# All rows for the attention's scores, and split activations on multiples of 512 bytes, in a two-layer hybrid decoder

## The chip, the cores and the metric

The kernel runs on one core of one Trainium2 chip. Times are device microseconds of one execution. A core has TensorE (PE: matmuls, and weight loads, PEld), VectorE (DVE), ScalarE (ACT), GpSimd (POOL) and SyncE (SP, which here only issues transfers). Each engine works through its own list of instructions in order and waits for others by semaphores.

## What is computed

Two layers, each of them three mixers over 512 tokens of width 1024 (x <- x + W_out(sum of gated projections)); the second mixer is the one whose scores change:

```python
def stick_breaking(q, k, v, q_norm, k_norm):          # 8 heads of 64, blocks of 128 queries
    q = rmsnorm(q, q_norm)
    k = rmsnorm(k, k_norm)
    for blk in range(S_ // SB_BLOCK):
        z = jnp.einsum('bqhd,bkhd->bhqk', q[:, start:end], k[:, :end]) * scale
        causal = s_idx[None, :] < t_idx[:, None]
        log_keep = jnp.where(causal, jax.nn.log_sigmoid(-z), 0.0)
        after = lax.cumsum(log_keep, axis=3, reverse=True) - log_keep
        w = jnp.where(causal, jnp.exp(jax.nn.log_sigmoid(z) + after), 0.0)
        outs.append(jnp.einsum('bhqk,bkhd->bqhd', w, v[:, :end]))

def hybrid_layer(x, ...):
    h = rmsnorm(x, norm_g)
    proj = h @ w_in                                    # 1024 x 8704, cut into 13 parts
    y_a = retention(...) * silu(rz);  y_b = stick_breaking(...) * silu(sz);  y_c = s5_ssm(...) * silu(cz)
    merged = sigmoid(ga) * (y_a @ proj_a) + sigmoid(gb) * (y_b @ proj_b) + sigmoid(gc) * (y_c @ proj_c)
    return x + merged @ w_out
```

## The kernel before

Large products are taken in a split form: a float32 value is the sum of a rounded float32r part (`hh`, `wh`, `yah`, ...) and the rest (`hl`, `wl`, `yal`, ...), and `three` (L336) adds the products high x high, high x low and low x high into one PSUM tile `mm`. The normalised, transposed input of a layer lies in two constant tiles, `hh` and `hl` (L235, L236; 128 partitions x 8 blocks x 512 tokens, so 16 KB of each partition). They are used in two ways:

- token-major (`token_major`, L351; `sq`, `sk`, `sv`, `cu`, `rq`, `rk`, `rv`): a block of 128 tokens of `hh` or `hl` is the stationary operand, a half of a weight tile `wh` or `wl` of 512 columns the moving one; 24 matmuls of 128x512 fill one tile. (`cu` takes every fourth token.)
- channel-major (`channel_major`, L371; gates `ga`, `gb`, `gc`, and `sz`, `cz`, `rz`): 128 columns of a weight are stationary, and the 512 tokens of `hh` or `hl` move; again 24 matmuls.

In the profile a matmul is named out<-moving,stationary, so `mm<-wh,hh` is token-major and `mm<-hh,wh` channel-major. The projections `pa`, `pb`, `pc` and the output product have tiles of the pool in place of `hh` and `hl` (`yah`, `ybh`, `ych`, `mgh`).

The program is written slot by slot: the table `ORDER_TEXT` gives the order of the main pieces, of 24 or 12 matmuls each, and small work (the attention's heads, the state-space quarters, the retention chunks) is put between the pieces by generators that say after how many slots they go on (`K`). Background work that builds the state-space tables is added by a running count of each engine's load.

An attention pair `sb_pair` (L1015) holds two heads of 64 rows each, one in partitions 0 to 63 and one in 64 to 127. Its first slot splits queries and keys: `qd` is the rounded query, copied by POOL to the other half of the partitions; `ks` holds the rounded key in the head's half and the key's rest in the other, so that one 128-row product `qd x ks` gives high x high plus high x low; `ql`, one tile for both heads, is the query's rest, and its product with the rounded key has 64 rows. `scores` (L1032) puts these two and a bf16 mask product (`identb x negm`) into PSUM; the first block (b = 0) takes one product of the unsplit float32 queries and keys over 64 rows, which PE runs as two instructions. Block 3 has a slot of its own (tile `z3`); blocks 0, 2 and 1 are one run in a later slot (`z02` and `z1`). Behind them ACT takes two sigmoids, DVE scans and multiplies (`weights_of`, L1043), and PE transposes the weights (`turn`, L1061, tile `wt`). The next pair's split comes in the slot of a pair's last run of three blocks.

The tiles of the large pool (`bt`, L216, 48 buffers of 2 KB) are handed out again as they come free.

Of the kernel before, what the change touches and what calls it, by code (L numbers as in the profile page):

```python
# [10 lines left out]
F32 = mybir.dt.float32  # L11
F32R = mybir.dt.float32r
BF16 = mybir.dt.bfloat16
AF = mybir.ActivationFunctionType
ALU = mybir.AluOpType
PSUM = bass.MemoryType.PSUM

P = 128
L = 2
S = 512  # L20
# [166 lines left out]
def trunk(ctx: ExitStack, tc, x_in, w_in, par_in, bc_in, ng_in, cst_in, rope_in, out):  # L187
    nc = tc.nc
    load = {"V": 0.0, "G": 0.0, "T": 0.0}

    def counted(f, engine, each):


        def g(*a, **k):
            o = k["out"] if "out" in k else a[0]
            load[engine] += 0.07 * (engine != "T") + each * math.prod(o.shape[1:])
            return f(*a, **k)  # L197

        return g

    TT = counted(nc.vector.tensor_tensor, "V", 1.04e-3)
# [4 lines left out]
    MM = counted(nc.tensor.matmul, "T", 0.42e-3)  # L206

    const = ctx.enter_context(tc.tile_pool(name="const", bufs=1))
# [7 lines left out]
    def bt(name, dt=F32, shape=(P, 512)):  # L216
        return bp.tile(list(shape), dt, tag="b", name=name)
# [7 lines left out]
    def psm(name):  # L225
        return ps_sm.tile([P, 512], F32, tag="sm", name=name)
# [3 lines left out]
    ident = const.tile([P, P], F32, name="ident")  # L230
    identb = const.tile([P, P], BF16, name="identb")
    negm = const.tile([P, P], BF16, name="negm")
    mhalf = const.tile([P, 32], F32, name="mhalf")
    zero1 = const.tile([P, 1], F32, name="zero1")
    hh = const.tile([P, 8, S], F32R, name="hh")  # L235
    hl = const.tile([P, 8, S], F32R, name="hl")  # L236
    x1 = dp.tile([S, D], F32, name="x1")

    def C(n):
# [7 lines left out]
        out=negm, in_=negm, pattern=[[1, P]], base=0, channel_multiplier=-1, compare_op=ALU.is_ge, fill=0.0  # L247
# [31 lines left out]
    def split(src, name, shape=(P, 512)):  # L279
        h = bt(name + "h", F32R, shape)  # L280
        l = bt(name + "l", F32R, shape)
        ACT(h, src, AF.Copy)  # L282
        TT(out=l, in0=src, in1=h.bitcast(F32), op=ALU.subtract)
        return h, l
# [523 lines left out]
    def layer(l, last, base):  # L808
# [206 lines left out]
        def sb_pair(pr):  # L1015
            w02, w3 = [None] * 2, [None] * 2
            qf, kf = sq[pr], sk[pr]
            half = [slice(0, 64), slice(64, 128)]

            qd = [bt("qd0", F32R), bt("qd1", F32R)]  # L1020
            ks = [bt("ks0", F32R), bt("ks1", F32R)]
            ql = bt("ql", F32R)
            for h in range(2):
                r, o = half[h], half[1 - h]
                ACT(qd[h][r, :], qf[r, :], AF.Copy)  # L1025
                ACT(ks[h][r, :], kf[r, :], AF.Copy)
                TT(out=ql[r, :], in0=qf[r, :], in1=qd[h][r, :].bitcast(F32), op=ALU.subtract)
                TT(out=ks[h][o, :], in0=kf[r, :], in1=ks[h][r, :].bitcast(F32), op=ALU.subtract)
                nc.gpsimd.tensor_copy(out=qd[h][o, :], in_=qd[h][r, :])  # L1029
            yield K["b1"]  # L1030

            def scores(ps, off, h, b):  # L1032
                n = 128 * (b + 1)
                c = slice(b * P, b * P + P)
                r = half[h]
                if b == 0:
                    MM(ps[:, off : off + n], qf[r, c], kf[r, 0:n], start=True, stop=False)
                else:
                    MM(ps[:, off : off + n], qd[h][:, c], ks[h][:, 0:n], start=True, stop=False)
                    MM(ps[:, off : off + n], ql[r, c], ks[h][r, 0:n], start=False, stop=False)  # L1040
                MM(ps[:, off + n - P : off + n], identb, negm, start=False, stop=True)

            def weights_of(ps, segs, sg):  # L1043

                end = sum(segs[-1])
                kp = bt("kp")
                ACT(kp[:, 0:end], ps[:, 0:end], AF.Sigmoid, scale=-0.125)  # L1047
                ACT(sg, ps[:, 0:end], AF.Sigmoid, scale=0.125)
                for off, n in segs:
                    v = kp[:, off + 1 : off + n][:, ::-1]  # L1050
                    nc.vector.tensor_tensor_scan(v, v, zero1.to_broadcast([P, n - 1]), 1.0, ALU.mult, ALU.add)  # L1051
                TT(out=sg[:, 0 : end - 1], in0=sg[:, 0 : end - 1], in1=kp[:, 1:end], op=ALU.mult)

            w1 = bt("w1")
            wt0, wt13, wt2 = [None] * 2, [None] * 2, bt("wt2")

            def wblk(h, b, kb):
                c = kb * P + (128 if b == 2 else 256 * h if b == 1 else 0)
                return (w02[h], w1, w02[h], w3[h])[b][:, c : c + P]

            def turn(h):  # L1061
                pts = []
                for blocks in (
                    [(b, 0) for b in range(4)], [(1, 1), (2, 1), (3, 1), (3, 3)], [(2, 2), (3, 2)],
                ):
                    pt = psm("wt")
                    for i, (b, kb) in enumerate(blocks):
                        nc.tensor.transpose(pt[:, i * P : i * P + P], wblk(h, b, kb), ident)
                    pts.append(pt)
                return pts  # L1070

            def turned(h, pts):
                wt0[h], wt13[h] = bt("wt0"), bt("wt13")
                ACT(wt0[h], pts[0], AF.Copy)
                nc.vector.tensor_copy(out=wt13[h], in_=pts[1])
                ACT(wt2[:, 256 * h : 256 * h + 256], pts[2][:, 0:256], AF.Copy)

            for h in range(2):
                ps = psm("z3")
                scores(ps, 0, h, 3)  # L1080
                if h == 1:
                    pts = turn(0)
                yield 0
                w3[h] = bt("w3")
                weights_of(ps, [(0, 512)], w3[h])
                if h == 1:
                    turned(0, pts)
                yield K["b2"]
                ps, ps1 = psm("z02"), psm("z1")
                scores(ps, 0, h, 0)  # L1090
                scores(ps, 128, h, 2)
                scores(ps1, 0, h, 1)
                yield 0
                w02[h] = bt("w02")
                weights_of(ps, [(0, 128), (128, 384)], w02[h])
                weights_of(ps1, [(0, 256)], w1[:, 256 * h : 256 * h + 256])
                yield K["b3"]
            pts = turn(1)
            yield 0
            turned(1, pts)  # L1100
            yield K["b4"]
            po = psm("sbo")
            for kb in range(4):

                for h in range(2):
                    c = slice(128 * pr + 64 * h, 128 * pr + 64 * h + 64)
                    w = (wt0[h], wt13[h][:, 0:384], wt2[:, 256 * h : 256 * h + 256], wt13[h][:, 384:512])[kb]
                    MM(po[half[h], 128 * kb : 512], sv[kb][:, c], w, start=kb == 0, stop=kb == 3)
            yield 0
            sbo[pr] = bt("sbo")  # L1110
            nc.vector.tensor_copy(out=sbo[pr], in_=po)
            yield K["b5"]
            while zb[pr] is None:
                yield 1
            TT(out=sbo[pr], in0=sbo[pr], in1=zb[pr], op=ALU.mult)
            yb[pr] = split(sbo[pr], "yb")
# [207 lines left out]
        for i in range(4):  # L1324
            spawn(sb_pair(i), at["sv"] + 3 + K["sb0"] + K["sb_gap"] * i)
# [66 lines left out]
```

## Time and profile before

| what | value |
|---|---|
| median of 3 runs (range) | 1330.12 us (1329.44 to 1330.89) |
| the profiled execution: its time, its span | 1332.1 us, 1330.4 us |
| PE busy | 1299.4 us, 98% |
| DVE busy | 854.5 us, 64% |
| ACT busy | 537.7 us, 40% |
| POOL busy | 371.3 us, 28% |
| PE clock granted, mean | 0.993 |

Busy time counts from an instruction's start to its end. PE's matmuls overlap each other, so their rows add up to more than the time they take; the distance from one start to the next is what a matmul costs in a stream. Idle time in front of a row is named with the engine that ended it. Buffer numbers are left out of names, so `z` stands for `z3`, `z02` and `z1`, `ks` for `ks0` and `ks1`, `sqk` for the unsplit queries and keys.

### The profile page before, as it was taken

The numbers are of one execution on the slowest core, as the hardware profiler recorded it, in microseconds if no ns is written. First come the engines' busy times: TensorE is split into PE (matmuls) and PEld (weight loads), VectorE is DVE, ScalarE is ACT, GpSimd is POOL, SyncE is SP. The second block draws the span as 40 slices with busy tenths as digits, with TensorE's granted clock in tenths as the row PEclk, the third lists the DMA queues.
The fourth block names the chain that finished last, engine by engine and source line by source line (L and its number), as shares of the span: only waits on it lengthen the run. The fifth ranks groups of instructions, "written<-read, shape, count | busy, mean of one in ns | idle before, by whom it ended". The sixth has DMA issues, their size and how long they took to land. (4 is left out here: it accounts for less than half of the span.)

```text
span 1330.4 us, 16615 instructions
## 1 busy us (share of the span) xinstructions
PE 1299.4 (98%) x6360; PEld 1051.4 (79%) x6360; DVE 854.5 (64%) x1189; ACT 537.7 (40%) x919; POOL 371.3 (28%) x436
## 2 busy tenths in 40 slices
PE   7989989999999999999999999899999999999998
PEld 5867768788887888888888777688888878888887
DVE  5996677886686438555365566779647854485542
ACT  5345543535434434333234444344544444333311
POOL 3330035738443012000052000575465321120000
PEclk9999989999999999999999999899999999999999
DMA  6232221223321222224533221112242233223342
GB/s 220 85 125 77 64 64 30 94 68 96 100 91 64 95 80 73 86 91 139 166 113 125 79 65 64 48 64 80 80 127 64 64 94 97 79 64 95 95 131 75
DMA packets 37375, 120.05 MB, mean 90 GB/s; under 512 B 4144, under 2 KB 4528, under 8 KB 37296
## 3 DMA queue, kind: packets, MB, share of 16 engines
q1 hardware_dynamic: 29664, 105.40, 25.2%
q10 hardware_dynamic: 7632, 13.59, 3.0%
q8 instruction: 50, 0.82, 0.3%
q14 instruction: 29, 0.24, 0.1%
HBM read 114.78 MB, written 4.19 MB: 89 GB/s over the span
## 5 line engine op out<-in xcount | busy, mean ns | idle before, releaser
L197 DVE TENSOR_TENSOR wl<-raw,wh 128x1024 fp32r<-128x1024 f32 x196 | 250.4, 1287 | 122.1 <-ACT wh L316 120.0
L197 PE MATMUL mm<-hh,wh 128*128 128x512 f32 x640 | 256.7, 401 | 0.0
L197 PE MATMUL mm<-hh,wl 128*128 128x512 f32 x640 | 252.4, 394 | 2.3 <-DVE wl L197 2.3
L197 PE MATMUL mm<-hl,wh 128*128 128x512 f32 x640 | 250.5, 391 | 0.0
L316 ACT ACTIVATE wh<-raw 128x1024 fp32r<-128x1024 f32 x196 | 206.0, 1057 | 86.1 <-DVE wl L197 31.1
L197 PE MATMUL mm<-wh,hh 128*128 128x512 f32 x512 | 210.2, 411 | 0.9 <-ACT hh L419 0.9
L197 PE MATMUL mm<-wl,hh 128*128 128x512 f32 x512 | 205.3, 401 | 4.1 <-DVE wl L197 4.1
L197 PE MATMUL mm<-wh,hl 128*128 128x512 f32 x512 | 204.7, 400 | 0.0
L197 PEld LDWEIGHTS mm<-hh,wl 128*128 128x128 f32 x640 | 120.6, 188 | 30.3 <-DVE wl L197 3.6
L197 PEld LDWEIGHTS mm<-hh,wh 128*128 128x128 f32 x640 | 120.8, 189 | 24.9 <-issue 1.8
L197 PEld LDWEIGHTS mm<-hl,wh 128*128 128x128 f32 x640 | 120.7, 189 | 24.5
L197 PEld LDWEIGHTS mm<-wl,hh 128*128 128x128 f32 x512 | 104.8, 205 | 25.7 <-DVE wl L197 6.8
L197 PEld LDWEIGHTS mm<-wh,hh 128*128 128x128 f32 x512 | 104.6, 204 | 21.3 <-ACT hh L419 1.3
L197 PEld LDWEIGHTS mm<-wh,hl 128*128 128x128 f32 x512 | 104.5, 204 | 20.9 <-DVE hl L197 0.3
L1051 DVE TENSOR_TENSOR_SCAN kp<-kp,zero 128x511 f32<-128x511 f32 (+1 forms) x64 | 60.3, 963 | 35.6 <-ACT kp L1047 35.1
L992 ACT ACTIVATE gate<-mm 128x512 f32<-128x512 f32 x48 | 28.6, 596 | 119.7 <-PE mm L197 119.7
L197 POOL TENSOR_SCALAR ms<-ss 128x8 f32<-128x8 f32 (+3 forms) x56 | 19.2, 342 | 184.0 <-DVE ss L822 101.9
L1029 POOL CAST qd<-qd 64x512 fp32r<-64x512 f32 x16 | 15.8, 988 | 186.9 <-ACT qd L1025 172.0
L197 POOL TENSOR_TENSOR rs<-ms,mhalf 128x8 f32<-128x8 f32 (+3 forms) x56 | 64.7, 1155 | 4.7
L820 ACT ACTIVATE sq<-mm 128x512 f32<-128x512 f32 x32 | 19.0, 593 | 89.1 <-PE mm L197 89.1
L197 PE MATMUL mm<-wl,mgh 128*128 128x512 f32 x128 | 50.1, 391 | 0.2
L197 PE MATMUL mm<-wh,mgh 128*128 128x512 f32 x128 | 49.9, 390 | 0.0
(254 smaller groups left out, 2260.4 us busy)
## 6 DMA issues: line engine op xcount, KB each, us to landing
raw<-in_w SPq DMA_DIRECT2D x196, 512.0 KB, 3.5
x<-in_x SPq DMA_DIRECT2D x8, 256.0 KB, 7.3
rope<-in_rope ACTq DMA_DIRECT2D x8, 256.0 KB, 4.3
xh<-in_x ACTq DMA_DIRECT2D x8, 256.0 KB, 4.6
x<-xh ACTq DMA_DIRECT2D x8, 256.0 KB, 2.1
xh<-x ACTq DMA_DIRECT2D x8, 256.0 KB, 4.5
out<-xh ACTq DMA_DIRECT2D x8, 256.0 KB, 2.1
gB<-in_ng SPq DMA_DIRECT2D x2, 256.0 KB, 5.8
```

The source lines that it names most:

```text
L197: return f(*a, **k)
L316: ACT(wh, raw, AF.Copy)
L820: ACT(s2, ps, AF.Square)
L992: ACT(sg, ps, AF.Sigmoid)
L1029: nc.gpsimd.tensor_copy(out=qd[h][o, :], in_=qd[h][r, :])
L1051: nc.vector.tensor_tensor_scan(v, v, zero1.to_broadcast([P, n - 1]), 1.0, ALU.mult, ALU.add)
```

## The change

Two things are done. First, `ql` becomes two tiles, one per head; POOL sets the half of each that the head doesn't use to zero, and all scores, those of block 0 too, are `qd x ks` and `ql x ks` over 128 rows. Second, two unused tiles are put among the constants, and `hh` and `hl` come ahead of the two small ones.

```diff
     negm = const.tile([P, P], BF16, name="negm")
+    const.tile([P, 152], F32, name="fill")
+    hh = const.tile([P, 8, S], F32R, name="hh")
+    hl = const.tile([P, 8, S], F32R, name="hl")
     mhalf = const.tile([P, 32], F32, name="mhalf")
     zero1 = const.tile([P, 1], F32, name="zero1")
-    hh = const.tile([P, 8, S], F32R, name="hh")
-    hl = const.tile([P, 8, S], F32R, name="hl")
+    const.tile([P, 104], F32, name="fill2")
...
-            ql = bt("ql", F32R)
+
+            ql = [bt("ql0", F32R), bt("ql1", F32R)]
             for h in range(2):
                 r, o = half[h], half[1 - h]
                 ACT(qd[h][r, :], qf[r, :], AF.Copy)
                 ACT(ks[h][r, :], kf[r, :], AF.Copy)
-                TT(out=ql[r, :], in0=qf[r, :], in1=qd[h][r, :].bitcast(F32), op=ALU.subtract)
+                nc.gpsimd.memset(ql[h][o, :].bitcast(F32), 0.0)
+                TT(out=ql[h][r, :], in0=qf[r, :], in1=qd[h][r, :].bitcast(F32), op=ALU.subtract)
...
-                r = half[h]
-                if b == 0:
-                    MM(ps[:, off : off + n], qf[r, c], kf[r, 0:n], start=True, stop=False)
-                else:
-                    MM(ps[:, off : off + n], qd[h][:, c], ks[h][:, 0:n], start=True, stop=False)
-                    MM(ps[:, off : off + n], ql[r, c], ks[h][r, 0:n], start=False, stop=False)
+                MM(ps[:, off : off + n], qd[h][:, c], ks[h][:, 0:n], start=True, stop=False)
+                MM(ps[:, off : off + n], ql[h][:, c], ks[h][:, 0:n], start=False, stop=False)
                 MM(ps[:, off + n - P : off + n], identb, negm, start=False, stop=True)
```

In the built program `hh` began at byte 18,496 of a partition and `hl` at 34,880, both 64 bytes past a multiple of 512; now they begin at 18,944 and 35,328, which are multiples of 512. The weight and activation pools lay 1,024 bytes past multiples of 2,048 and now lie on multiples of 2,048; multiples of 512 they were before, too.

On PE, the run of blocks 0, 2 and 1 of the first head of layer 1 (`z_1054` and `z_1059` are the tile of blocks 0 and 2). Before:

```order
L197 MATMUL z_1054<-sqk 128x128
```

and now:

```order
L197 MATMUL z_1059<-ks_949,qd_947 128x128
L197 MATMUL z_1059<-ks_949,ql_951 128x128
```

Every run of three blocks, 16 in all, has these two in place of the one; the rest of PE's list stands as it was, with `ql` read over 128 rows.

On POOL, the quarter of the state-space tables in which block products with `ccr` and `cci` are built (`ct`, then `ca`, then the copies `b` and the cleared `mt`); what an instruction waits for stands behind it. Before:

```order
L197 TENSOR_TENSOR ct_1930<-ccr,y_re 128x512 [waits PE_49]
L197 TENSOR_TENSOR ct_1931<-cci,y_im 128x512 [waits Pool_49]
L197 TENSOR_TENSOR ca<-ct_1930,ct_1931 128x4x128 [waits Pool_49]
L763 COPY b_1997<-bbr 64x256
L763 COPY b_1997<-bbi 64x256 [waits Pool_49]
```

and now:

```order
L197 TENSOR_TENSOR ct_1951<-ccr,y_re 128x512 [waits PE_49,Activation_49]
L197 TENSOR_TENSOR ct_1952<-cci,y_im 128x512 [waits DVE_49]
L197 TENSOR_TENSOR ca<-ct_1951,ct_1952 128x4x128 [waits Pool_49]
L765 COPY b_2018<-bbr 64x256 [waits DVE_49]
L765 COPY b_2018<-bbi 64x256 [waits Pool_49]
```

The order is the same; the second `ct` and the first `b` have other buffers than before, which DVE has to release. In POOL's list 16 memsets are new, each directly ahead of the copy of `qd` of the same head.

## Rows read from the trace of the kernel before

**Rows 1.** The page, busy time of PE: us, share of the span, instructions.
```profile
PE 1299.4 (98%) x6360; PEld 1051.4 (79%) x6360; DVE 854.5 (64%) x1189; ACT 537.7 (40%) x919; POOL 371.3 (28%) x436
```
**Rows 2.** PE's waits: who waited for whom, us in total, times, longest.
```profile
PE wt L1068 <- DVE w L197: 8.1, 4, 2.4
PE mm L197 <- DVE wl L197: 6.3, 7, 1.5
PE z L197 <- DVE ks L197: 2.7, 1, 2.7
```
**Rows 3.** PE's timeline, blocks 0, 2, 1 of a head: start us, us, operation.
```profile
180.50 0.40 PE L197 MATMUL mm<-hh,wl 128*128 128x512 f32 x1
...
181.28 0.42 PE L197 MATMUL z<-ks,qd 128*128 128x384 f32 x1
181.63 0.44 PE L197 MATMUL z<-ks,ql 64*128 64x384 f32 x1
...
182.65 0.23 PE L197 MATMUL z<-negm,identb 128*128 128x128 bf16 x1
...
183.01 0.40 PE L197 MATMUL mm<-hl,wh 128*128 128x512 f32 x1
```
**Rows 4.** PE's timeline, block 3 of the other head; in brackets idle time, releaser.
```profile
188.28 0.40 PE L197 MATMUL z<-ks,qd 128*128 128x512 f32 x1
188.61 0.50 PE L197 MATMUL z<-ks,ql 64*128 64x512 f32 x1
189.04 0.23 PE L197 MATMUL z<-negm,identb 128*128 128x128 bf16 x1
...
193.64 1.76 PE L1068 MATMUL wt<-ident,w 128*128 128x128 f32 x7 [2.41 <-DVE w L197]
```
**Rows 5.** The chain that ended last: start us, us from start to next, instructions.
```profile
1078.62 5.60 PE mm L197 x24
...
1112.27 0.89 PE rs L197 x8
...
1124.16 0.72 PE ro L197 x6
...
1192.03 5.50 PE mm L197 x24
...
1233.57 49.08 PE mm L197 x216
```
**Rows 6.** Timelines of DVE and PE behind the first pair's last scores.
```profile
123.46 0.42 DVE L197 TENSOR_TENSOR w<-w,kp 128x255 f32<-128x255 f32 x1
...
124.29 1.26 PE L1068 MATMUL wt<-ident,w 128*128 128x128 f32 x10
```
**Rows 7.** The page, costliest groups of PE: count | busy us, mean ns | idle.
```profile
L197 PE MATMUL mm<-wh,hh 128*128 128x512 f32 x512 | 210.2, 411 | 0.9 <-ACT hh L419 0.9
...
L197 PE MATMUL mm<-wh,mgh 128*128 128x512 f32 x128 | 49.9, 390 | 0.0
...
L197 PE MATMUL mm<-hh,wh 128*128 128x512 f32 x640 | 256.7, 401 | 0.0
L197 PE MATMUL mm<-hl,wh 128*128 128x512 f32 x640 | 250.5, 391 | 0.0
```
**Rows 8.** POOL's groups with shapes apart: the nearest memset.
```profile
L767 POOL MEMSET mt<- 128x512 f32 x16 | 7.9, 526 | 0.5
```
**Rows 9.** Timelines of POOL, DVE and PE at a quarter of the tables.
```profile
212.39 1.51 POOL L197 TENSOR_TENSOR ct<-cci,y_im 128x512 f32<-128x512 f32 x1
...
216.44 0.75 POOL L763 COPY b<-bbi 64x256 f32<-64x256 f32 x1
...
216.97 0.77 DVE L197 TENSOR_TENSOR Ti<-ct,ct 128x512 f32<-128x512 f32 x1
...
224.13 0.64 PE L197 MATMUL pk<-ca,b 128*32 128x128 f32 x16
```
**Rows 10.** Stretch: us, busy of PE, PEld, DVE, ACT, POOL, PE clock, DMA.
```profile
188.00:196.00 8.00, 3.93 (x16) 2.96 (x16) 7.70 (x6) 3.26 (x6) 6.83 (x6) 0.80 0.22 66
```

## The prediction

> **What bounds the kernel now.** I read the page's busy table first: TensorE (PE) is busy 1299 us of the span of 1330 [rows 1]. A busy PE is not a PE at its peak, so next came its waits: besides the start these are the transposes of the attention's weights (`wt`, 8.1 us in all), the layer's products `mm` (6.3 us) and the first scores `z` of layer 1 (2.7 us), all waiting for VectorE (DVE) [rows 2]. So nearly every nanosecond taken from a PE instruction shortens the span, except just before those waits. After that I read PE's start-to-start times in the timeline, since each matmul starts before the one ahead has drained: the length of a row is not its cost, the distance to the next start is.
>
> **The scores, as they stand.** For a head the blocks 0, 2 and 1 are one run of PE work. From the start of the last `mm` ahead (180.50) to the start of the second `mm` behind (183.01) are 2.51 us [rows 3]; two `mm` of 0.227 us (price below) are not the scores', so the run costs 2.05 us. Inside it every change between a 128-row and a 64-row product shows as lost time: the 384-column product over 128 rows begins at 181.28 and the one over 64 rows behind it only at 181.63, 0.35 us later. Block 3 is a second run: its 512-column product starts at 188.28, the 64-row one at 188.61, the mask at 189.04, so two products take 0.76 us [rows 4]. Both runs come 16 times (2 layers, 4 pairs, 2 heads).
>
> **What they cost with all rows.** Now all products have 128 rows and nothing is switched inside a run. Prices by column count come from the chain of work that ended last, in which PE instructions follow each other without a gap: 512 columns 0.227 us, 256 columns 0.72/6 = 0.12 us, 128 columns 0.89/8 = 0.11 us [rows 5]; 384 columns lie between, about 0.17 us. A mask costs what 182.65 to 183.01 leaves after one `mm`, 0.13 us [rows 3], less where the product ahead is short; I take 0.11 us. The run of three blocks is then 2 x 0.11 + 2 x 0.17 + 2 x 0.12 + 3 x 0.11 = 1.13 us, 0.92 us less, x16 = **14.7 us**. Block 3 is 2 x 0.227 in place of 0.76 us: 0.30 us less, x16 = **4.8 us**. Raw sum 19.5 us.
>
> The unknown price is the 128-column product of float32r, of which the trace has none. Below: at the rate of the 512-column row it streams in 0.06 us, which would gain another 32 x 0.05 = 1.6 us; above: a four-byte float32 product of 128 columns is two instructions of 0.11 us [rows 5], and if float32r needs both, 32 x 0.11 = 3.5 us are lost. I take 0.11 us, since that row is such an instruction, with a load of the same size in front.
>
> **What of it is lost again.** The weights' transposes wait for DVE's chain behind the scores. Where the next pair's split comes in between, this chain starts with ScalarE's work on the `mm` piece that ends before the scores, so shorter scores do not shorten it. In the third such place PE already waits (193.64, after 2.41 us) [rows 4]: the whole 1.2 us goes, in both layers, 2.4 us. In the first such place DVE ends `w` at 123.88 and PE starts `wt` at 124.29 [rows 6]: 0.4 us of cover, so 0.8 us is lost there, and the same in the second; four in all, 3.2 us. The stop at layer 1's first `z` takes 0.3 us, and later `mm` stops for `wl` [rows 2] I put at 0.6 us. Scores net: 19.5 - 6.5 = **13 us**.
>
> **The places of `hh` and `hl`.** In token-major products these are the stationary operand, in channel-major ones the moving one. A token-major piece of 24 takes 5.60 us, 0.2333 each; a channel-major piece 5.50 us, 0.2292 each; the 216 that follow are one such piece and 192 products of the `pa` projection, whose operands all lie on multiples of 512 bytes: (49.08 - 5.50)/192 = 0.2270 each [rows 5]. The mean durations lean the same way: 411 ns with stationary `hh`, 390 with stationary `mgh`, 401 with moving `hh` [rows 7]. There are 3 x 512 token-major and 3 x 640 channel-major products on `hh`, `hl`. At full effect: 1536 x 6.3 ns = 9.7 us and 1920 x 2.2 ns = 4.2 us. PE's gain on `sk`, `sq` and `sv` of layer 1 (288 products, 1.8 us) ends at the DVE wait before the first `z`, and some 100 products before the `wl` stops of each layer give 1.2 us more away. Of the 10.9 us left I take three quarters, **8 us**, because the `pa` stretch is long and unbroken, while pieces on `hh` are often cut by transposes, behind which the pace need not be as good. Ends: nothing, and 11 us.
>
> For the size of this a page of the Trainium skill can be set beside the row. Even the `pa` row keeps 0.227 us for 512 columns [rows 5]. TensorE: Matmul & The Clock Gate, section "Back-to-back issue gap", gives N/2.4 + 2.5 ns, 0.216 us for 512 columns at the full clock; if alignment brought that, an estimate from this page, the gain would be 1536 x 17 + 1920 x 13 ns = 51 us. The aligned products of this trace do not run so, and I follow the row.
>
> **What is added.** GpSimd (POOL) gets 16 memsets of 64 x 512. The nearest row is a memset of 128 x 512 at 0.53 us [rows 8]; POOL stands idle before most of the copies beside which they come, and nobody waits for POOL's copies. Cost 0, at most 16 x 0.5 = 8 us were POOL the bound. DVE's and ScalarE's lists do not change. The second `ql` takes one more buffer of the pool per pair, so later tiles get other buffers: in the quarter of the state-space tables that stands at 212.39 [rows 9], POOL's `ct` now reuses a buffer that DVE reads until 217.74. POOL stops there for up to 5.4 us, with `ca`, `b` and `mt` queued behind it, and PE's `pk` (224.13) waits for these. From 212.39 to the end of `b` (217.19) are 4.8 us; begun at 217.74 they end at 222.5, 1.6 us ahead of `pk`, and PE comes earlier by about the 1.2 us of a head's scores. I take 0; both layers have the place.
>
> **Sum.** 13 + 8 = 21 us. The profiled execution took 1332.1 us (span 1330.4, 1.7 around it), 2 us above the median of the runs, 1330.1; I take the difference from both, and forecast **1309 us** for the median.
>
> **Rivals.**
> - *Alignment does nothing.* `hh` and `hl` differ from the `pa` operands in more than the offset: they lie in another part of the memory, and the matmuls around them differ. For it: a moving `hl` shows no loss, 391 ns against 401 for `hh` at the same offset [rows 7]. Then only the scores count: 1330 - 13 = 1317 us. SBUF — State Buffer, section "Specifications (TRN2)" in the Trainium skill, speaks for this rival: full rate needs two hits per 16-byte line, and 64 bytes past a boundary is the start of such a line. No run here shows the lines by themselves.
> - *The scores' gain stays in DVE's chains.* If the other weights' transposes, too, have less cover than I think, half the scores' gain goes: 1330 - 6 - 8 = 1316; with alignment at nothing 1324 us. Against: PE stops for `w` in few places [rows 2].
> - *Slower: POOL's new stop reaches PE.* If `pk` waits, PE stands still, and behind a stop of this size the granted clock falls: in the 8 us around the stop at 189 it is 0.80, where the levels are 1.2 and 2.4 GHz [rows 10]. A stop of 5.4 us in each layer with some 2 us of low clock costs 15 us. That ends slower only where alignment gives nothing and the scores give under 12 us: 1330 - 12 + 15 = 1333 us. It decides from 6 us of stop per layer on. Against: the copies to be waited for end before `pk` even with the stop.
>
> **How the numbers follow.** Forecast 0.60 (1309), alignment nothing 0.22 (1317), chains 0.12 (1316 to 1324), slower 0.03 (1333), no effect of size 0.03. Range: from 1303 (alignment 11, scores 13, the short products at 0.06 us, and a little less lost) to 1321 (alignment nothing, short products at the dear price 1317 + 3.5). A measurement here tells about 0.2% (2.7 us) from no change. Faster 0.94, same 0.03, slower 0.03.
>
> **What would show it.** The distance from the last `mm` ahead of a three-block run to the second behind should fall from 2.51 to about 1.6 us, and no 0.35 us step between products should remain; 128-column products starting 0.21 us apart would be the dear price. A token-major piece should take 5.45 us in place of 5.60, a channel-major one 5.46 in place of 5.50. The stop at 193.64 should be longer by about 1 us, and new short waits of `wt` for `w` should appear. A wait of `pk` for POOL, or a slower `pa`, would prove me wrong; unchanged 5.60 would make the first rival's case, and a fall well below 5.45 would mean that more than the offset cost time.

## The result, and the profile after

The changed kernel takes **1310.67 us** (median of 4 runs, 1309.67 to 1311.17) against 1330.17 us for the kernel before on the same chip: a ratio of 0.985, 95% interval 0.9835 to 0.987, or 19.5 us less. The forecast was 1309 us. The profiled execution has a span of 1309.5 us.

The page of the changed kernel, busy time, answers to [rows 1].

```profile
PE 1271.7 (97%) x6360; PEld 1048.5 (80%) x6360; DVE 855.6 (65%) x1189; ACT 537.6 (41%) x919; POOL 382.5 (29%) x452
```

PE's waits (who waited for whom, us in total, times, longest) answer to [rows 2].

```profile
PE wt L1068 <- DVE w L197: 13.5, 8, 3.1
PE mm L197 <- DVE wl L197: 9.2, 7, 3.3
PE T L398 <- DVE xn L197: 9.0, 2, 7.4
PE mm L197 <- ACT hh L421: 0.9, 1, 0.9
PE z L197 <- DVE ks L197: 0.8, 1, 0.8
```

PE is busy 28 us less and waits more: its waits were 26.9 us in all and are now 33.4 us. `wt` now waits for `w` in 8 places, not 4, and for 5.4 us more. So PE's own work fell by more than the time did, and part of it came back as waiting.

PE's timeline of the changed kernel at the first run of blocks 0, 2 and 1 of layer 1 (start us, us, operation) answers to [rows 3], which show a later run of the kernel before:

```profile
99.75 0.39 PE L197 MATMUL mm<-hh,wl 128*128 128x512 f32 x1
99.98 0.22 PE L197 MATMUL z<-ks,qd 128*128 128x128 f32 x1
100.03 0.28 PE L197 MATMUL z<-ks,ql 128*128 128x128 f32 x1
100.15 0.23 PE L197 MATMUL z<-negm,identb 128*128 128x128 bf16 x1
100.19 0.42 PE L197 MATMUL z<-ks,qd 128*128 128x384 f32 x1
100.45 0.34 PE L197 MATMUL z<-ks,ql 128*128 128x384 f32 x1
...
100.99 0.23 PE L197 MATMUL z<-negm,identb 128*128 128x128 bf16 x1
101.03 0.48 PE L197 MATMUL mm<-hh,wh 128*128 128x512 f32 x1
101.35 0.40 PE L197 MATMUL mm<-hl,wh 128*128 128x512 f32 x1
```

From 99.75 to 101.35 are 1.60 us, where 2.49 to 2.51 stood before, depending on the run. The 384-column product over 128 rows is followed by the next one 0.26 us later, in place of 0.35. The two products of 128 columns start 0.06 us apart.

PE's timeline at the place of [rows 4], a block 3 with the transposes of the attention's weights behind it (idle time and its releaser in brackets); this is the third such place of layer 1:

```profile
181.93 0.39 PE L197 MATMUL z<-ks,qd 128*128 128x512 f32 x1
...
182.39 0.23 PE L197 MATMUL z<-negm,identb 128*128 128x128 bf16 x1
185.68 0.30 PE L1068 MATMUL wt<-ident,w 128*128 128x128 f32 x1 [3.07 <-DVE w L197]
188.40 2.18 PE L1068 MATMUL wt<-ident,w 128*128 128x128 f32 x9 [2.41 <-DVE w L197]
```

Two products take 0.46 us in place of 0.76. The first `wt` now starts 3.30 us behind the mask. Before it was 1.89 us (the mask at 189.04 in [rows 4], `wt` at 190.93):

```profile
190.93 0.30 PE L1068 MATMUL wt<-ident,w 128*128 128x128 f32 x1 [1.66 <-DVE w L197]
```

So this stop is 1.4 us longer; the second stop, the one that [rows 4] show, kept its 2.41 us.

The chain that ended last (start us, us to the next, instructions) answers to [rows 5]:

```profile
1058.78 5.49 PE mm L197 x24
...
1171.24 5.49 PE mm L197 x24
...
1212.72 49.02 PE mm L197 x216
```

One of the page's groups (count, busy us, mean ns, idle) answers to [rows 7]:

```profile
L197 PE MATMUL mm<-wh,hh 128*128 128x512 f32 x512 | 207.5, 405 | 0.9 <-ACT hh L421 0.9
```

The token-major piece at 1058.78 went from 5.60 to 5.49 us, the channel-major one at 1171.24 only from 5.50 to 5.49 (other channel-major pieces of the chain fell further, see below); the 192 products of `pa` behind a piece of 24 still take (49.02 - 5.49)/192 = 0.2267 us each. With stationary `hh` the mean duration fell from 411 to 405 ns.

### The profile page after: what moved, and what is told of

The parts are those of the page before. It is cut to its first block, busy times and chain, and to the rows that moved or that the text cites. A ratio compares the mean times of both kernels' runs of the same rounds, so it can differ in the third digit from the quotient of the medians.

```text
span 1309.5 us, 16640 instructions
## 1 busy us (share of the span) xinstructions
PE 1271.7 (97%) x6360; PEld 1048.5 (80%) x6360; DVE 855.6 (65%) x1189; ACT 537.6 (41%) x919; POOL 382.5 (29%) x452
## 5 line engine op out<-in xcount | busy, mean ns | idle before, releaser
L197 PE MATMUL mm<-wh,hh 128*128 128x512 f32 x512 | 207.5, 405 | 0.9 <-ACT hh L421 0.9
L197 PE MATMUL mm<-wl,hh 128*128 128x512 f32 x512 | 202.6, 396 | 4.3 <-DVE wl L197 4.3
L197 PE MATMUL mm<-wh,hl 128*128 128x512 f32 x512 | 202.0, 395 | 0.0
L1051 DVE TENSOR_TENSOR_SCAN kp<-kp,zero 128x511 f32<-128x511 f32 (+1 forms) x64 | 67.6, 1076 | 26.2 <-ACT kp L1047 26.1
```

## The experiments

Each run is compared with runs of the kernel before on the same chip (medians of 1330.0, 1330.0 and 1331.1 us in the three groups of runs, 1330.2 beside the changed kernel). Where a run is set against the changed kernel instead, these differences of up to 1 us stand between the two.

### The two halves alone

`e_scores` has the second half of the diff only, `e_place` the first only:

```diff
 e_scores
-            ql = bt("ql", F32R)
+            ql = [bt("ql0", F32R), bt("ql1", F32R)]
...
 e_place
+    const.tile([P, 152], F32, name="fill")
+    hh = const.tile([P, 8, S], F32R, name="hh")
+    hl = const.tile([P, 8, S], F32R, name="hl")
...
+    const.tile([P, 104], F32, name="fill2")
```

> The scores' change alone: all products over 128 rows, hh and hl where they were (64 bytes past a multiple of 512). Theory (two gains that add): the scores are worth 11 to 13 us net, so 1317 to 1319 us; three-block runs last 1.60 us, a token-major piece of 24 stays at 5.60 us and a channel-major one at 5.50. Rival (the scores did nearly all, and the place of hh and hl only adds waits later): 1312 us or less. Rival (most of the scores' gain is lost before DVE's chains, and the places carry the result): 1322 us or more.

> The places of hh and hl alone (18,944 and 35,328), scores as before. Theory: the token-major piece falls to 5.49 us, the channel-major one by 0.01, together 8 us: 1322 us. Rival (alignment does nothing by itself): 1329 to 1331 us. If e_scores and this one together give clearly more than 19.5 us, the two parts compete for the same waits; if less, they help each other.

Measured: the scores alone 1316.87 us (1316.46 to 1318.41; ratio 0.9905, interval 0.989 to 0.9919), 13.2 us less than before; the places alone 1322.81 us (1322.06 to 1324.12; ratio 0.9948, interval 0.9933 to 0.9963), 7.2 us less. Together 20.4 us, where the whole change gave 19.5: the halves add up to within 1 us, and both of the forecast's terms, 13 and 8, hold.

### Which operand's place counts, and by how much

The forecast read the loss as "64 bytes past a multiple of 512" and left open that the region of memory or the neighbours were the cause. Six runs move the tiles of the changed kernel by a few bytes and change nothing else: `fill` moves `hh` and `hl`, and `fill2` takes up the difference or, where it doesn't, moves all tiles of the pools (weights, `yah`, `mgh` and so on). The diff is that of `e_off32`; the others have other numbers in these two lines (first column of numbers in the table below).

```diff
-    const.tile([P, 152], F32, name="fill")
+    const.tile([P, 160], F32, name="fill")
...
-    const.tile([P, 104], F32, name="fill2")
+    const.tile([P, 96], F32, name="fill2")
```

> The changed kernel with hh and hl moved by 64 bytes (19,008 and 35,392), everything else at the same addresses. Theory (the offset from a multiple of 512 costs the time): token-major pieces return to 5.60 us, channel-major to 5.50, and the time is that of the scores alone, 1317 to 1319 us. Rival (the part of the memory, or the order of the constants, made the difference): pieces stay at 5.49 and the time at 1311 us.

> The changed kernel with hh and hl moved by 256 bytes (19,200 and 35,584), everything else at the same addresses. If only multiples of 512 are good: as with 64 bytes, 1317 to 1319 us, token-major pieces 5.60 us. If a smaller grain, of 128 or 256 bytes, is what counts: 1311 us and 5.49 us as in the changed kernel.

> The changed kernel with the second unused tile 64 bytes longer: hh and hl stay on multiples of 512, every tile of the pools (weights, attention and projection operands) begins 64 bytes past one. Nothing is left out. Theory that the offset counts for any operand of TensorE, as the stationary or the moving one: all products slow by 2 to 6 ns, the pa stretch of 216 from 49.0 to 50 us or more, 4300 products of mm by about 4 ns give 17 us, about 1325 to 1330 us. Rival (only the token-major stationary operand is sensitive, because of its place or of the 2048-byte distance between its rows): 1311 us and the pa stretch at 49.0.

> The changed kernel with the first unused tile 128 bytes longer and the second 128 bytes shorter: hh and hl begin 128 bytes past a multiple of 512, all other tiles where they were. Nothing is left out. At 64 bytes past, the time was 1318.3, at 256 past 1311.1. If the grain is 128 bytes: 1311 us and a token-major piece of 24 at 5.49. If it is 256 bytes: 1318 us and 5.60. In between (one boundary in two is crossed): 1314 us and 5.54.

> The changed kernel with hh and hl 32 bytes past a multiple of 512, all other tiles where they were. Nothing is left out. At 64 bytes the time was 1318.3 (token-major piece 5.59, channel-major 5.50), at 128 bytes 1322.9 (5.58 and 5.60). If the loss grows with the distance: 1314 us, token-major 5.54. If any distance that is no multiple of 256 costs the same to the stationary side: 1317 to 1319 us, 5.59. If only steps of 64 bytes count: 1311 us.

> The changed kernel with the first unused tile 64 bytes longer: hh, hl and every tile of the pools begin 64 bytes past multiples of 512, so that stationary and moving operands have the same offset again. Nothing is left out. Theory of the absolute offset (each operand must lie on a multiple of 256 or 512): the losses of the two runs with one side displaced add up, 1318.3 - 1310.7 = 7.6 and 1321.8 - 1310.7 = 11.1 us, about 1329 us, a token-major piece 5.62, a channel-major one 5.62. Theory of the relative offset (what counts is how far the moving operand's place modulo 256 bytes is from the stationary one's; the pa stretch, displaced as a whole in the run with displaced pools, did not slow): 1311 us and pieces of 5.49.

Measured, with the token-major piece and the channel-major pieces of 24 (shortest to longest) from the chain that ended last; the last two columns are the place of the stationary operand less that of the moving one, modulo 256 bytes (`cu`, which takes every fourth token, apart):

| run | `fill`, `fill2` | time, us (range) | token-major, us | channel-major, us | distance, token | distance, channel |
|---|---|---|---|---|---|---|
| changed kernel | 152, 104 | 1310.67 (1309.67 to 1311.17) | 5.49 | 5.46 to 5.49 | 0 | 0 |
| `e_off256` | 216, 40 | 1311.07 (1309.94 to 1311.73) | 5.49 | 5.46 to 5.49 | 0 | 0 |
| `e_all64` | 168, 104 | 1310.80 (1309.80 to 1312.09) | 5.47 | 5.46 to 5.50 | 0 | 0 |
| `e_off64` | 168, 88 | 1318.31 (1317.12 to 1318.44) | 5.59 | 5.50 to 5.60 | +64 | -64 |
| `e_pool64` | 152, 120 | 1321.80 (1320.91 to 1322.26) | 5.51 | 5.59 to 5.63 | -64 | +64 |
| `e_off128` | 184, 72 | 1322.87 (1321.41 to 1323.57) | 5.58 | 5.58 to 5.60 | 128 | 128 |
| `e_off32` | 160, 96 | 1323.03 (1322.77 to 1324.62) | 5.60 | 5.58 to 5.61 | +32 | -32 |

The chain that ended last in `e_off64`, a token-major piece and two channel-major ones:

```profile
1064.74 5.59 PE mm L197 x24
...
1132.85 5.60 PE mm L197 x24
...
1178.16 5.50 PE mm L197 x24
```

The same in `e_pool64`, with the 216 products that hold `pa`:

```profile
1067.50 5.51 PE mm L197 x24
...
1181.24 5.59 PE mm L197 x24
...
1223.55 49.21 PE mm L197 x216
```

And in `e_all64`:

```profile
1059.33 5.47 PE mm L197 x24
...
1171.77 5.47 PE mm L197 x24
...
1213.22 49.03 PE mm L197 x216
```

`e_off64` has the constants in their new order and region, and only the 64 bytes back: it loses 7.6 us, as much as the places had brought by themselves (7.2). So the byte offset is the cause and not the region, and the forecast's first rival falls. `e_off256` shows that 256 does as well as 512.

`e_pool64` brought the turn, with a time that neither of its two theories had given. The pools' tiles are displaced, `hh` and `hl` are not, and now the channel-major piece, whose stationary operand is the weight, is the slow one. But the 192 products of `pa`, whose operands are *both* displaced, take (49.21 - 5.60)/192 = 0.2271 us, as good as ever. That speaks against a rule for each operand by itself, and `e_all64` was made to decide: with everything displaced by 64 bytes the time is 1310.8 us, where two separate losses would have given 1329. **What counts is the distance between the stationary and the moving operand modulo 256 bytes, not the place of either.** In the chain a piece takes 5.46 to 5.50 us at a distance of 0, 5.59 to 5.63 at +64, and 5.58 to 5.61 at 128 and at 32 on either side. At -64 most pieces take 5.50 or 5.51, but one channel-major piece of the same chain takes 5.60.

All products on `hh` and `hl` in the traces, and not only those of the chain, say how much that is. The table has the mean distance from start to start, in ns, of products of one kind that follow each other directly (distances under 300 ns; some 1400 token-major and 1770 channel-major ones in each run, `cu` among them):

| run | token-major | channel-major |
|---|---|---|
| before | 233.9 (at +64) | 229.3 (at -64) |
| changed kernel | 228.8 (at 0) | 228.0 (at 0) |
| `e_all64` | 228.7 (at 0) | 227.6 (at 0) |
| `e_off64` | 233.9 (at +64) | 229.3 (at -64) |
| `e_pool64` | 230.4 (at -64) | 233.3 (at +64) |
| `e_off128` | 233.5 (at 128) | 232.9 (at 128) |
| `e_off32` | 233.9 (at +32) | 233.3 (at -32) |

So -64 is not free: it costs some 1.5 ns for each product, where +64, 128 and 32 on either side cost some 5 ns. Why the sign counts at 64 and not at 32, and why single pieces at -64 are as slow as those at +64, stays open. My expectations for 128 and 32 bytes missed: no value was offered above that of 64 bytes, yet both are some 4.5 us slower, because there the channel-major pieces pay in full as well.

The Trainium skill, SBUF — State Buffer, section "Specifications (TRN2)", which stood with the first rival, counts 16-byte lines; 32 and 64 bytes are whole numbers of these, and the runs show a loss at both, so its rule doesn't describe this one. What in the chip makes the distance count wasn't found. The mean duration of a weight load (LDWEIGHTS) doesn't show it: 204 ns for `mm<-wh,hh` in the changed kernel, 205 in `e_off64`.

### Where the scores' gain lies

`e_blk0` is the changed kernel with block 0 as before, so that one switch from 128 to 64 rows and back is left in a run. `e_group` puts all `ql` products back to 64 rows, but the three of a run next to each other:

```diff
 e_blk0
+                if b == 0:
+                    r = half[h]
+                    MM(ps[:, off : off + n], qf[r, c], kf[r, 0:n], start=True, stop=False)
+                else:
...
 e_group
+                r = half[h]
+                if lo and b:
+                    MM(ps[:, off : off + n], ql[h][r, c], ks[h][r, 0:n], start=True, stop=False)
+                if hi:
+                    MM(ps[:, off : off + n], qd[h][:, c], ks[h][:, 0:n], start=b == 0, stop=False)
+                    MM(ps[:, off + n - P : off + n], identb, negm, start=False, stop=b > 0)
+                if lo and b == 0:
+                    MM(ps[:, off : off + n], ql[h][r, c], ks[h][r, 0:n], start=False, stop=True)
...
                 scores(ps, 0, h, 0)
-                scores(ps, 128, h, 2)
-                scores(ps1, 0, h, 1)
+                scores(ps, 128, h, 2, hi=False)
+                scores(ps1, 0, h, 1, hi=False)
+                scores(ps, 128, h, 2, lo=False)
+                scores(ps1, 0, h, 1, lo=False)
```

> The changed kernel with block 0 of the scores as it was before: one float32 product of 64 rows, two instructions, in the middle between the 384- and the 256-column products of 128 rows; the second product of the other blocks stays at 128 rows. Nothing is left out. By the trace of the changed kernel the two 128-column products and their mask take 0.26 us in the run of three blocks. If the scores' gain is the switching between 64 and 128 rows, the run of three goes from 1.60 back by two switches, to about 1.9 to 2.0 us, and 16 such runs cost 5 to 6 us, of which two thirds show: 1314 to 1315 us. If the gain lies in the two longer products of ql alone (64-row loads not hidden), block 0 costs no more than the columns it streams: 1311 us and a run of 1.6 to 1.7 us.

> The changed kernel with the ql products over the head's 64 rows again, but ordered so that the three of a run stand next to each other (block 0's behind its mask, then those of blocks 2 and 1, then the 128-row products of blocks 2 and 1), and in block 3 ahead of the 128-row one. Nothing is left out. In the changed kernel the run takes 1.60 us. If it is the switch between 64 and 128 rows that costs, about 0.3 us for going there and back as in the kernel before, the run takes 1.85 to 1.95, one excursion in place of three. If it is the 64-row product itself (its load is not hidden), each of the three costs again: 2.2 to 2.5 us. The whole time follows damped by the stops of wt: 1312 to 1314 by the first, 1317 to 1319 by the second.

PE's timeline at the first run of three in `e_blk0`:

```profile
99.44 0.39 PE L197 MATMUL mm<-hh,wl 128*128 128x512 f32 x1
99.76 0.49 PE L197 MATMUL z<-sqk 64*128 64x128 f32 x2
...
101.38 0.40 PE L197 MATMUL mm<-hl,wh 128*128 128x512 f32 x1
```

And in `e_group`:

```profile
99.70 0.39 PE L197 MATMUL mm<-hh,wl 128*128 128x512 f32 x1
...
100.15 0.67 PE L197 MATMUL z<-ks,ql 64*128 64x128 f32 x3
...
101.64 0.39 PE L197 MATMUL mm<-hl,wh 128*128 128x512 f32 x1
```

One excursion to 64 rows costs a run 0.34 us in `e_blk0` (1.94 against 1.60) and, with three products in it, 0.33 us in `e_group` (1.93 by the unrounded starts). Before there were three excursions and 0.91 us: the price is that of going there and back, about 0.3 us, whether block 0's one product (two instructions) is made there or three. So the switch was the main cost, as the forecast had read from the 0.35 us step; a 64-row product by itself is a small part.

In the whole time the two runs differ. `e_group` takes 1318.13 us (1316.84 to 1318.74). My expectation of 1312 to 1314 had priced the runs of three and forgotten block 3, which has its excursion back, too: 0.39 us longer in the trace, from the start of the `mm` ahead to that of the mask. That makes 16 x (0.33 + 0.39) = 11.5 us of PE work for 7.5 us of time. `e_blk0` takes 1311.97 us (1310.60 to 1313.60), 1.3 more than the changed kernel, with ranges that overlap (0.4 if each is set against the kernel before on its own chip), for 16 x 0.34 = 5.4 us more PE work. I had expected 1314 to 1315, two thirds of that work in the time. Its waits fell by 4.4 us, from 33.4 to 29.0, `wt` for `w` from 13.5 to 9.6. The row of PE's waits in `e_blk0`:

```profile
PE wt L1072 <- DVE w L197: 9.6, 8, 2.2
```

So most of what the change brings at block 0 is lost again at PE's waits, nearly all of it in front of `wt`. That leads to the last question.

### Taking the lost part back

The chain on DVE that makes the weights starts with the next pair's split. `e_early` moves the split of the later pairs one slot ahead in the changed kernel, `e_bearly` does the same in the kernel before:

```diff
-            yield K["b1"]
+            yield K["b1"] + (pr > 0)
...
-            spawn(sb_pair(i), at["sv"] + 3 + K["sb0"] + K["sb_gap"] * i)
+            spawn(sb_pair(i), at["sv"] + 3 + K["sb0"] + K["sb_gap"] * i - (i > 0))
```

> The changed kernel, with the split of the second, third and fourth pair of a layer moved one slot ahead, so that it no longer stands between a pair's last scores and the chain on VectorE that makes their weights. Nothing is left out. Theory (a part of the scores' gain was lost because the chain behind the scores starts with the next pair's split and not with the scores): the stops of the transposes wt for w, 13.5 us in all in the changed kernel, fall below 4 us, and the time falls by 8 to 10 us to about 1302 us. Rival (these stops come from VectorE being busy with other work that is only shifted, so that the wait comes up elsewhere, at the scores, at mm for wl or at the next wt): the sum of PE's waits stays near 33 us and the time at 1310 to 1312 us.

> The kernel before with the later pairs' split one slot earlier, as in the run that took 1301.0 us, and nothing else. Nothing is left out. If that run's further 9.7 us were gain of the scores that the chain behind them had kept back, the same edit gives less here, where the stops of wt for w are 8.1 us and not 13.5: 1324 to 1326 us. If the edit is worth its 9.7 us by itself, 1320 us.

Measured: `e_early` **1301.02 us** (1299.33 to 1301.51; ratio to the kernel before 0.9775, interval 0.9761 to 0.9788), 9.7 us less than the changed kernel (10.5 if each is set against the kernel before on its own chip). `e_bearly` 1323.67 us (1322.77 to 1326.69; ratio 0.9956, interval 0.9943 to 0.997), 6.3 us less than the kernel before. PE's wait for `w` in `e_early`:

```profile
PE wt L1068 <- DVE w L197: 5.4, 4, 2.0
```

The four new short waits are gone, and the long stop in the third place is 1.99 and 0.74 us in place of 3.07 and 2.41; the sum of 5.4 us is not below 4, as I had expected. That third place is a case of its own. DVE's timeline in the changed kernel, first at the first place, then at the third:

```profile
118.50 1.27 DVE L1051 TENSOR_TENSOR_SCAN kp<-kp,zero 128x127 f32<-128x127 f32 x2
119.87 0.69 DVE L197 TENSOR_TENSOR w<-w,kp 128x511 f32<-128x511 f32 x1
...
181.07 3.06 DVE L1051 TENSOR_TENSOR_SCAN kp<-kp,zero 128x127 f32<-128x127 f32 x2
184.24 1.30 DVE L197 TENSOR_TENSOR w<-w,kp 128x511 f32<-128x511 f32 x1
185.46 1.54 DVE L1051 TENSOR_TENSOR_SCAN kp<-kp,zero 128x255 f32<-128x255 f32 x1
```

POOL's timeline at the third place:

```profile
182.05 1.27 POOL L197 TENSOR_TENSOR ab<-ab,ct 128x512 f32<-128x512 f32 x1
183.29 1.70 POOL L197 TENSOR_TENSOR ab<-bbr,y_re 128x512 f32<-128x512 f32 x1
184.95 1.50 POOL L197 TENSOR_TENSOR ct<-bbi,y_im 128x512 f32<-128x512 f32 x1
```

And the timelines of POOL and DVE at the third place in `e_early`:

```profile
179.25 2.15 POOL L197 TENSOR_TENSOR ab<-ab,ct 128x512 f32<-128x512 f32 x1
...
180.18 2.40 DVE L1051 TENSOR_TENSOR_SCAN kp<-kp,zero 128x127 f32<-128x127 f32 x2
182.68 0.69 DVE L197 TENSOR_TENSOR w<-w,kp 128x511 f32<-128x511 f32 x1
183.29 0.68 DVE L1051 TENSOR_TENSOR_SCAN kp<-kp,zero 128x255 f32<-128x255 f32 x1
```

In the first place POOL's list is empty during the scans and two of them take 1.27 us; in the third POOL multiplies state-space tables at the same time, and the same two take 3.06 us, the product behind them 1.30 in place of 0.69. (So it was in the kernel before: 3.10 and 1.30 us.) In `e_early` POOL's multiplications end at 181.4, and what DVE does behind that has its usual length, 0.68 for the scan of 255 columns in place of 1.54. Nor is that all: behind the long stop the granted clock is low. A stretch of 8 us from the end of the stop on in the changed kernel (us, busy of PE, PEld, DVE, ACT, POOL, PE clock, DMA):

```profile
188.00:196.00 8.00, 7.60 (x28) 7.00 (x29) 5.22 (x6) 0.98 (x2) 1.66 (x3) 0.67 0.20 66
```

The same in `e_early`:

```profile
183.50:191.50 8.00, 7.24 (x36) 7.03 (x36) 5.59 (x7) 1.05 (x3) 0.00 (x0) 1.00 0.41 133
```

0.67 is a mixture of the two levels, 1.2 and 2.4 GHz; 1.00 is the higher one throughout. PE had stood still for 3.07 and 2.41 us ahead of the first stretch, and for 1.99 and 0.74 ahead of the second. But the length of the stops doesn't settle the clock by itself: in layer 2 of `e_early` they are the same, 1.98 and 0.74 us, and the clock of the 8 us behind them (821 to 829) is 0.79.

The gains can be separated by the distance in PE's timeline from the start of a block 3 to the start of the run of three behind it. Where no `wt` waits, it is 7.10 us in the changed kernel. At the first short wait it was 7.53 us before and is 7.95 in the changed kernel (8.01 at the second) and 7.10 again in `e_early`. At the third place it was 14.94 us in layer 1 and 14.33 in layer 2 before; it is 15.37 and 15.12 in the changed kernel, 10.50 and 11.93 in `e_early` (the second of these with the clock of 0.79). The stops of the layer-1 place are 2.75 us shorter in `e_early`, its distance 4.87 us, so some 2 us of the gain there come from behind the stops, where the clock is higher. These places also vary from run to run: in `e_place`, with the scores as before, they take 13.63 and 14.15 us. So `e_early` gets 2 x (0.85 + 0.91) = 3.5 us back at the four short waits and 8.1 us at the third places; some 1 us it gives back at layer 1's first scores and ahead of the third places. In `e_bearly` the short places stay at 7.53, and the third one falls to 10.48 in both layers, which is 8.3 us.

So both accounts in the expectations hold in part. About 3.4 us, the difference of the two edits (9.7 - 6.3, with some 2 us of spread in the runs; 4.2 if each is set against its own chip), fit the 3.5 us at the four short waits: gain of the scores that the chain had kept back. The other 6.3 us are an improvement at the third place that the kernel before could have had as well.

## Why the prediction was right, and where it wasn't

- **The scores, raw.** 2.51 to about 1.6 us was forecast, and 1.60 stands there; block 3 went from 0.76 to 0.46 as forecast. 16 x (0.91 + 0.30) = 19.4 us against 19.5.
- **The 128-column product and the mask.** The distance of the first pair is 0.06 us, the lower bound, and 0.12 from the second to the mask; I took 0.11 for each. The next instruction starts 0.04 us behind a mask, not 0.11, but that next one then takes 0.08 or 0.09 longer than its price: 0.26 for the 384 columns over `qd` in place of 0.17, and 0.32 for the `mm` at 101.03 in place of 0.227. So a mask costs 0.12 to 0.13 in all, a little more than the forecast took, the two products of 128 columns 0.17 and not 0.22, and the two errors cancel in the 1.60.
- **What is lost again.** For the scores 6.5 us was forecast; 19.4 - 13.2 = 6.2 us is what `e_scores` lost. That PE's waits also grew by 6.5 us in the whole change, from 26.9 to 33.4, is in part luck: in `e_scores` they are 30.7, only 3.8 more. By the distances from block 3 to the run behind it, `e_scores` loses 3.3 us at the four short places and 2.1 us at the two third ones, 5.4 of the 6.2. In the changed kernel the four short places lost 0.85 and 0.91 us each by the distances above (0.8 forecast), and new waits of `wt` stand there as said. The stop in the third place grew by 1.4 us (1.2 forecast), but it was the first of its two stops and not the one at 193.64, which was to grow and kept its 2.41 us. `mm` for `wl` grew by 2.9 us, more than the 0.6 I had, but at the start of layer 1 that is the stop ahead of the first `z` (2.7, now 0.8 us) moved a few products on: together 9.0 us became 10.0. The net of 13 us was measured as 13.2.
- **The places: size right.** 8 us forecast, 7.2 measured. By the means above a token-major product gained 5.1 ns (6.3 in the forecast) and a channel-major one 1.3 (2.2), so 1536 x 5.1 + 1920 x 1.3 ns = 10.3 us, three quarters of the 9.7 + 4.2 us at full effect. So the cut to three quarters had the right size, and the reason that it was given fits the traces: in the changed kernel 32 pieces of 24 have no other work in between, and 24 times the mean distance in them is 5.44 us in 26 of them, as good as the 0.2270 us of the `pa` row, and 5.47 in the others; products beside other work are slower. Some 3 us were to be lost at stops, and 3.1 of the 10.3 are missing from the time; but in `e_place` PE's waits are 27.3 us, only 0.4 more than before, so where they went isn't shown. The chain's last section, from which both prices came, shows less for channel-major pieces, 5.50 to 5.49, than the rest of the kernel does.
- **The places: reason wrong.** The forecast took from the `pa` stretch that its operands lie on multiples of 512. They also lie at the same place *as each other*, and `e_all64` shows that it is this that counts. In the kernel before, one displacement stood between `hh` and everything it met; any fix that removes the difference modulo 256 would have done. That multiples of 512 were the right place for `hh` and `hl` is luck in this sense: the pools lay on such multiples, too. It also explains why the rows of channel-major products spoke for the rival: with `hh` or `hl` moving, the distance was -64 bytes, which costs some 1.5 ns and not 5. The mean of moving `hh`, 401 ns in [rows 7], had nothing to do with the place; it is 400 in the page of the changed kernel:

```profile
L197 PE MATMUL mm<-hh,wh 128*128 128x512 f32 x640 | 256.0, 400 | 0.0
```

- **POOL.** The new stop at `ct` came, 5.64 us (5.4 forecast), and reached nobody: the second `b` ends at 215.11, one microsecond ahead of `pk`, which has no idle time in front of it; in layer 2 it is the same (857.11 and 858.11). The memsets take 0.52 us each and no engine waits for them. POOL's timeline:

```profile
209.83 1.44 POOL L197 TENSOR_TENSOR ct<-cci,y_im 128x512 f32<-128x512 f32 x1 [5.64 <-DVE Ti L197]
...
214.30 0.81 POOL L765 COPY b<-bbi 64x256 f32<-64x256 f32 x1
```

POOL's group of the memsets (count, busy us, mean ns, idle before):

```profile
L1030 POOL MEMSET ql<- 64x512 f32 x16 | 8.3, 521 | 33.6 <-issue 23.0 <-PE wt L1068 9.9
```

PE's timeline:

```profile
216.10 0.65 PE L197 MATMUL pk<-ca,b 128*32 128x128 f32 x16
```

- **The rivals.** That alignment does nothing is refuted by `e_place` and `e_off64`. That half of the scores' gain stays in DVE's chains is refuted for the whole (13.2 net of 19.4), though for block 0 taken alone it is what happened (`e_blk0`). The slower case didn't come.

## What to carry to other kernels

Compare the places of the *two* operands of a matmul, not each with a boundary: keep the difference of their start addresses at a multiple of 256 bytes, best by putting all large tiles on the same offset. Going to 64 rows and back between products over 128 rows cost 0.3 to 0.4 us here, whether one product was made there or three, so pad with zeros, or gather such products. And when PE is made faster ahead of a wait, look at where the waiting chain starts: here one slot was worth 9.7 us more, half of what the change itself brought, though 6.3 of these could have been had before the change.

## What was not expected of the hardware

- The distance rule above: 512-column products of float32r lost some 5 ns each (233.9 in place of 228.8 ns, token-major) by 32, +64 or 128 bytes between the operands, and some 1.5 ns by -64. Other types and shapes were not tried.
- DVE's scan takes more than twice its time beside POOL's multiplications (3.06 against 1.27 us for two, 1.54 against 0.68 for the one of 255 columns), and the stop of `wt` behind it is the longest. The Trainium skill, GPSIMD Engine Reference, section "1. Specifications", says that POOL shares its SBUF interfaces with DVE and contends with DVE instructions of two SBUF inputs; the scans and products here are such, and the trace agrees.
- Two 128-column products of float32r behind a 512-column one start 0.06 us apart, while the 128-column float32 instructions of [rows 5] stand 0.11 us apart in a stream.
